# A layer with window attention, a two-way scan and memory attention: the hand-over of key tiles, the order of the last period and the rests of the side tasks

## The chip, the cores and the metric

The kernel runs on one core of one Trainium2 chip. The core has a matmul engine (TensorE, PE in the profile), a vector engine (VectorE, DVE), an engine for activation functions (ScalarE, ACT), a general one (GpSimd, POOL) and SyncE (SP), whose queue issues all of this kernel's DMA transfers. The metric is the time on the device in microseconds, from the start to the end of one launch; lower is better.

## What is computed

One encoder layer over 2048 tokens of width 1024, in float32, with three groups of heads side by side: window attention (16 query heads in 4 groups, each group with one key head), a Mamba-2 scan in both directions, and attention into 256 memory tokens.

```python
proj = rms_norm(h) @ w_in           # q, k, v, gates, z, xbc, dt, memory queries and gates
q, k = rotary(q), rotary(k)
att  = window_attention(q, k, v, sink) * silu(g_attn)      # blocks of 128 queries, keys within +-128
xbc  = silu(centred_depthwise_conv(xbc))                   # 5 taps
dt   = softplus(dt_raw + dt_bias)
y    = ssd_scan(forward) + ssd_scan(backward) + d_skip * xs
ssd  = gated_group_rmsnorm(y, z)
mem  = softmax(q_mem @ mk.T / sqrt(128)) @ mv * silu(g_mem)
h    = h + concat[att, ssd, mem] @ w_out
return rms_norm(h)
```

## The kernel before

The 2048 tokens are cut into 4 periods of 512, each of 4 blocks of 128, and worked from period c = 3 down to c = 0. The projections carry most of the matmul work. A float32 product is made as three products of a rounded high part and a low rest (`split3`: xh with wh, xl with wh, xh with wl; PE takes the rounded type `float32r` faster than float32). `split` makes the two parts, the high one on ACT (L174), the low one on DVE (L175). Weights come tile by tile through `ws` into `wh` and `wl`.

PE's order is written by the program itself, by a small planner that runs while the kernel is built. The main line (`main`) emits projections. Everything else is a *task*, a generator that emits some instructions and then yields a number, its rest. The planner keeps a clock: each matmul adds an estimate (0.216 us for a 512-column one of float32r), each transpose 0.11. After every second matmul group of the main line `tick` runs all tasks whose rest is over. `need(...)` holds the main line back until certain tasks are done: then tasks follow one another on PE without projections between them, and the planner's clock jumps ahead. There are five kinds of tasks: "att" (three at once), "mem", "ssd", "inc" and "fwd" (one each). The order on the other engines and on SP is not written by hand: a scheduler takes it from its own forecast of the times.

In a period the main line makes keys (`keys`, with the rotary step `rope`) and values, then for each head group g its query heads (`heads`), conv projections (`conv`), the gate of the scan (`z_gate`) and the memory heads (`mem_project`).

- `heads` projects the two query halves, rotates them (`rope`), writes them to DRAM (`q_d`) and reads them back in another layout into the tile `qs`; then it projects two gates, and spawns one `attention` task for each of the 4 blocks.
- `attention`: block 4c takes a place for the key tiles, starts their loads (`khh`, `kll`, `vg`), hands them to the other blocks of the group (`kv["t"]`, L498) and rests 9.0. The others wait in a loop until `kv["t"]` is there. Then each block makes 4 pairs of score matmuls into 2 banks (`s`), which DVE empties at L512 (mask, sink and row maximum `mx`); ACT takes exponentials (L520) and scales (L524). After a rest of 14.0 (9.0 for group 3 of the last period) come transposes (`t`), and 3.0 later the product with the values (`o`).
- `mem_project` loads the memory keys `mkt` and spawns `mem_attention`, which loads the memory values into the same tile once its scores are done.
- `ssd_local` makes the scan's work inside blocks, for both directions, and stores y and states. When it is done for all periods, `forward` runs block by block: it adds the state from before the block, which `incoming` prepares (`fb`, L713, L716), to y (tile `b`), multiplies by the gate (POOL, L736 and L738), squares (ACT, L739), adds pairs (DVE, L741) and rests 15.0. Then matmuls `t<-ones` make the sums (L745), DVE and POOL the factors (L747, L748, L751); after a rest of 4.0 the matmul `t<-yo` spreads them (L754), DVE scales (L756) and the block is stored to `mix_d`. The next step's `b` is the same tile.
- In the last period (c = 0) the main line makes all eight convs first and spawns `ssd_local`; then for g = 0 to 2 the memory head, the heads and one z gate, then heads 3, memory head 3 and the last z gate.
- Then the output projection: `early(c)` makes, for a block, the half of it that needs no scan, and puts it away to DRAM (`xr_d`). It is called from block 15 downward, as long as attention tasks are left. `rest_wo` loads the last seven rows of tiles of `w_out`. `out_block(c)` makes what is left of every block from 0 upward, and needs `forward(c)`.

Of the kernel before, what the change touches and what calls it, by code (L numbers as in the profile page):

```python
# [10 lines left out]
F32 = mybir.dt.float32  # L11
F32R = mybir.dt.float32r
# [24 lines left out]
def as32(ap):  # L37
    return ap.bitcast(F32)


def as32r(ap):
    return ap.bitcast(F32R)
# [3 lines left out]
def layer(ctx: ExitStack, tc: tile.TileContext, a: dict):  # L46
# [162 lines left out]
    def rope(pa, pb, tab):  # L209

        n = tab.shape[-1]
        t, u = (misc.tile([P, 2, CH], F32, name=f"rt{i}")[:, :, :n] for i in range(2))
        nc.vector.tensor_tensor(t, pa.unsqueeze(1).broadcast_to([P, 2, n]), tab[:, 1:3], ALU.mult)
        nc.vector.tensor_tensor(u, pb.unsqueeze(1).broadcast_to([P, 2, n]), tab[:, 0:2], ALU.mult)
        nc.vector.tensor_tensor(t, t, u, ALU.add)
        hi = as32r(misc.tile([P, 2, CH], F32, name="rt1")[:, :, :n])
        split(hi, as32r(t), t)
        return hi, as32r(t)
# [161 lines left out]
    def steps(s, nb, raw):  # L380
# [35 lines left out]
        nc.vector.tensor_tensor(wl, wl, dt.rearrange("p b d r -> p (b d r)"), ALU.mult)  # L416
        yield 1.5
        pt = bank(ps_t, "t")
        nc.tensor.transpose(pt[:n, :P], fl, ident)
        nc.vector.tensor_scalar(fl, fl, -1.0, None, ALU.mult)  # L420
# [60 lines left out]
    def attention(c, g, i, qs, gt, kv):  # L481
# [7 lines left out]
        if i == 4 * c:  # L489
            yield from take("kst", 1)  # L490
            kst = [ap_.tile([P, 6 * P], F32R, name=nm, bufs=2) for nm in ("khh", "kll")]
            for j in range(2):
                for u in range(2):
                    nc.sync.dma_start(as32(kst[j])[u * 64:(u + 1) * 64, :(hi + 1 - lo) * P],
                                      k_d[j, g * 32:(g + 1) * 32, :, lo * P:(hi + 1) * P].rearrange("p j t -> (p j) t"))
            vg = ap_.tile([P, 6, 64], F32, name="vg", bufs=2)
            nc.sync.dma_start(vg[:, :hi + 1 - lo], v_d[lo:hi + 1, :, g * 64:(g + 1) * 64].rearrange("b p d -> p b d"))
            kv["t"] = kst, vg  # L498
            yield 9.0
        yield from take("pm", 4)  # L500
# [22 lines left out]
        for r in range(4):  # L523
            nc.scalar.activation(pm[:, r, :w], pm[:, r, :w], AF.Copy, scale=den[:, r:r + 1])  # L524
        yield 14.0 if c or g < 3 else 9.0
        yield from take("pt", nk)
# [106 lines left out]
    def mem_project(c, xs, hd):  # L633
# [11 lines left out]
        nc.sync.dma_start(as32(mkt), mk_d[hd])  # L645
        return spawn("mem", mem_attention(c, hd, qh, ql, gm, mkt))

    def mem_attention(c, hd, qh, ql, gm, mkt):
        yield 11.0
        pms = []  # L650
        for half in range(2):
# [16 lines left out]
            pms.append(pm)  # L668
            if half:
                mvt = mkt.rearrange("p (u m d) -> p u m d", u=2, m=2)  # L670
                nc.sync.dma_start(as32(mvt), mv_d[:, :, :, hd * P:(hd + 1) * P].rearrange("u m p d -> p u m d"))
            yield 2.0 if half == 0 else 10.0
# [9 lines left out]
        for m, (tt, hi) in enumerate(pts):  # L682
            lo = misc.tile([P, 512], F32R, name="mpm", bufs=2)
            nc.vector.tensor_tensor(lo, tt, as32(hi), ALU.subtract)
            pts[m] = tt, hi, lo
        yield 2.0
        oo = bank(ps_o, "o")
# [6 lines left out]
    def incoming(c):  # L694
# [11 lines left out]
        for u in range(2):  # L706
            nc.sync.dma_start(ef[u * 64:(u + 1) * 64], ev[u].partition_broadcast(64))
        yield 5.0
        for d, st_ in enumerate((state["f"], hbt)):
# [4 lines left out]
            if d == 0:  # L714
                yield 1.0
        nc.gpsimd.tensor_tensor(ef[:, 0], ef[:, 0], ef[:, 1], ALU.add)  # L716
# [6 lines left out]
    def forward(c):  # L723
# [17 lines left out]
        nc.vector.tensor_tensor(zv[:, :, 0], zv[:, :, 0], zv[:, :, 1], ALU.add)  # L741
        yield 15.0
        pn = bank(ps_t, "t")
# [6 lines left out]
        for g in range(2):  # L750
            nc.vector.tensor_scalar(dg[:, g], ident, rn[:, g:g + 1], None, ALU.mult)  # L751
        yield 4.0
        pn = bank(ps_t, "t")
# [110 lines left out]
    fwd = []  # L864
    nz = [0] * NPER
    for c in range(NPER - 1, -1, -1):
        if c < NPER - 1:
            main(keys(c, xs))
            main(values(c, xs))
        if c == 0:  # L870
            for i in range(8):
                main(conv(c, xs, i))
            ssd_t = spawn("ssd", ssd_local(range(3, -1, -1)))
        tab = tables(CH * c, CH)
        for g in range(NG):
# [6 lines left out]
            elif c < NPER - 1:  # L882
                need(*att[c + 1, g + 2])
            if c == 0 and g < 3:
                need(mem_t)
                mem_t = main(mem_project(c, xs, g))
            att[c, g] = main(heads(c, xs, g, tab))
            if c and g == 2:
                norm_x(c - 1, rows_x(c - 1, dg))
            if c:  # L890
                main(conv(c, xs, 2 * g))
                main(conv(c, xs, 2 * g + 1))
                if g == 3:
                    spawn("ssd", ssd_local(range(4 * c + 3, 4 * c - 1, -1)))
            for _ in range(1 if c else ((1, 1, 1, 0))[g]):
                main(z_gate(c, xs, nz[c]))
                nz[c] += 1
            if c:
# [3 lines left out]
        if c == 0:  # L902
            need(mem_t)
            mem_t = main(mem_project(c, xs, 3))
            for i in range(nz[c], NG):
                main(z_gate(c, xs, i))
            fwd = [spawn("fwd", forward(b)) for b in range(NB)]
# [104 lines left out]
    while not all(t.done for ts in att.values() for t in ts):  # L1012
        if last < 4:
            need(*[t for ts in att.values() for t in ts])
        else:
            main(early(last))
            last -= 1
    rest_wo()
    for c in range(NB):
        main(out_block(c))  # L1020
# [70 lines left out]
```

## Time and profile before

| | |
|---|---|
| median of 3 runs | 1881.1 us (1878.0 to 1883.5) |
| the profiled execution | 1887.0 us, its span 1885.3 us |
| PE busy | 1770.2 us (94% of the span), 9242 matmuls |
| DVE busy | 1183.9 us (63%) |
| ACT busy | 925.1 us (49%) |
| POOL busy | 263.9 us (14%) |
| DMA (SP's queue) | 59.2% of 16 engines' span, 339.6 MB |
| mean granted clock of PE | 0.972 |

The span is the time from the first to the last instruction. Matmuls overlap, so a row's duration is longer than the distance from one start to the next. In a row of the timeline, what stands in brackets is how long the engine was idle before that instruction, and what released it. The granted clock is a share of 2.4 GHz; the clock has two levels, 2.4 and 1.2 GHz, and a mean between 1 and 0.5 is a mixture of them.

### The profile page before, as it was taken

How to read it: one execution, taken by the hardware profiler on the slowest of the kernel's cores; microseconds unless marked ns; L12 is line 12 of the kernel's file. 1: busy time of each engine (PE TensorE's matmuls, PEld its weight loads, DVE VectorE, ACT ScalarE, POOL GpSimd, SP SyncE). 2: the span in 40 equal slices, each digit the busy share in tenths (PEclk: the TensorE clock that was granted, in tenths of full speed). 3: DMA queues.
4: the chain of work that ended last, by engine and by line, in shares of the span. 5: the costliest groups of instructions: out<-in, count | busy, mean ns of one | idle time of the engine just before them, and what ended most of it. 6: DMA issues, size and time to landing. Idle time of an engine off the chain costs nothing.

```text
span 1885.3 us, 26616 instructions
## 1 busy us (share of the span) xinstructions
PE 1770.2 (94%) x9242; PEld 1441.6 (76%) x9242; DVE 1183.9 (63%) x2669; ACT 925.1 (49%) x1985; POOL 263.9 (14%) x253
## 2 busy tenths in 40 slices
PE   6789999998999999989999998999898989999998
PEld 6777878876778777866778787777676778888876
DVE  7456666686666668767576679866777543344332
ACT  6246546563756457456556665465566421111111
POOL 0000000012110000211000012211122233333220
PEclk9899999999999999999999999999999999999999
DMA  6746374577664755766474566655667765555442
GB/s 233 220 147 203 110 236 130 153 231 234 212 183 136 222 157 163 246 196 206 135 209 142 166 199 204 219 171 155 204 176 207 244 168 168 169 173 160 136 140 79
DMA packets 262695, 341.31 MB, mean 181 GB/s; under 512 B 29344, under 2 KB 171808, under 8 KB 262560
## 3 DMA queue, kind: packets, MB, share of 16 engines
q1 hardware_dynamic: 262560, 339.61, 59.2%
q8 instruction: 73, 1.20, 0.3%
q14 instruction: 62, 0.51, 0.1%
HBM read 251.20 MB, written 88.34 MB: 180 GB/s over the span
## 4 chain that ended last, share of the span: by engine, by line
PE 67%; DMA 14%; DVE 11%; ACT 4%; issue 3%; POOL 1%; SPq 1%; DVEq 0%; POOLq 0%; ACTq 0%
PE pj L156 50%; PE s L156 7%; PE o L156 5%; PE t L160 4%; DMA qs<-q_d 3%; DVE wl L175 2%; DMA q_d<-rt 2%; DMA cu<-in_x_dram 1%; DMA fb<-ef_d 1%; ACT wh L174 1%; DMA ws<-in_w_in_dram 1%; DMA mxl<-mix_d 1%; PE t L156 1%; DMA mix_d<-b 1%; DVE pm L512 1%
## 5 line engine op out<-in xcount | busy, mean ns | idle before, releaser
L156 PE MATMUL pj<-xh,wh 128*128 128x512 f32 (+2 forms) x1296 | 507.5, 392 | 1.6 <-ACT msq L852 1.6
L156 PE MATMUL pj<-xl,wh 128*128 128x512 f32 (+2 forms) x1296 | 495.9, 383 | 1.9 <-DVE xl L175 1.9
L156 PE MATMUL pj<-xh,wl 128*128 128x512 f32 (+2 forms) x1296 | 495.4, 382 | 0.1
L156 PEld LDWEIGHTS pj<-xh,wl 128*128 128x128 f32 x1296 | 247.5, 191 | 46.1 <-DVE wl L175 1.0
L156 PEld LDWEIGHTS pj<-xh,wh 128*128 128x128 f32 x1296 | 247.9, 191 | 40.9 <-issue 4.8
L156 PEld LDWEIGHTS pj<-xl,wh 128*128 128x128 f32 x1296 | 248.0, 191 | 36.8 <-DVE xl L175 2.4
L175 DVE TENSOR_TENSOR wl<-ws,wh 128x1024 fp32r<-128x1024 f32 (+2 forms) x175 | 211.4, 1209 | 96.1 <-ACT wh L174 89.5
L174 ACT CAST wh<-ws 128x1024 fp32r<-128x1024 f32 (+2 forms) x175 | 179.8, 1028 | 139.5 <-PE pj L156 96.9
L512 DVE CUSTOM_DVE_ANT_0 pm<-s,band,sink 128x384 f32<-128x384 f32 (+1 forms) x256 | 148.9, 594 | 68.6 <-PE s L156 66.9
L520 ACT ACTIVATE pm<-pm,mx 128x385 f32<-128x385 f32 (+1 forms) x256 | 151.2, 594 | 64.4 <-DVE mx L518 64.2
L608 POOL TENSOR_TENSOR b<-nat,win 128x256 f32<-128x256 f32 x64 | 44.3, 711 | 912.9 <-ACT nat L594 912.9
L156 PE MATMUL pj<-woh,mxh 128*128 128x512 f32 x416 | 171.4, 412 | 0.0
L156 PE MATMUL pj<-wol,mxh 128*128 128x512 f32 x416 | 166.1, 399 | 0.0
L156 PE MATMUL pj<-woh,mxl 128*128 128x512 f32 x416 | 166.1, 399 | 0.0
L156 PE MATMUL s<-khh,qs 128*128 128x384 f32 (+1 forms) x256 | 97.2, 380 | 55.0 <-DMA qs<-q_d 28.7
L524 ACT ACTIVATE pm<-pm,den 128x384 f32<-128x384 f32 (+1 forms) x256 | 132.9, 593 | 14.7 <-DVE den L522 14.7
L174 ACT CAST mxh<-mxl 128x512 fp32r<-128x512 f32 x64 | 39.6, 619 | 198.4 <-DMA mxl<-mix_d 94.9
L538 ACT COPY pt<-t 128x512 f32<-128x512 f32 x120 | 69.8, 582 | 103.7 <-PE t L160 103.5
L156 PEld LDWEIGHTS s<-khh,qs 128*128 128x128 f32 x256 | 50.3, 196 | 82.6 <-issue 35.1
L452 DVE SCALAR_TENSOR_TENSOR cu<-raw,cw,cu 128x512 f32<-128x512 f32 (+2 forms) x128 | 98.7, 778 | 15.6 <-ACT cu L450 14.5
L175 DVE TENSOR_TENSOR mxl<-mxl,mxh 128x512 fp32r<-128x512 f32 x64 | 50.4, 788 | 89.9 <-ACT mxh L174 89.8
L160 PE MATMUL t<-ident,pm 128*128 128x128 f32 x736 | 101.1, 274 | 2.7 <-ACT pt L538 1.8
(217 smaller groups left out, 2948.1 us busy)
## 6 DMA issues: line engine op xcount, KB each, us to landing
ws<-in_w_in_dram SPq DMA_DIRECT2D x152, 512.0 KB, 4.2
q_d<-rt SPq DMA_DIRECT2D x32, 512.0 KB, 5.5
qs<-q_d SPq DMA_DIRECT2D x32, 512.0 KB, 6.3
fb<-f_d SPq DMA_DIRECT2D x32, 512.0 KB, 4.6
mxl<-mix_d SPq DMA_DIRECT2D x64, 256.0 KB, 3.8
mix_d<-ao SPq DMA_DIRECT2D x64, 128.0 KB, 3.7
xc<-xbc_d SPq DMA_DIRECT2D x32, 256.0 KB, 3.8
st_d<-carry SPq DMA_DIRECT2D x32, 256.0 KB, 4.0
```

The costliest lines, as they stand in the source:

```text
L156: nc.tensor.matmul(out, lhsT=lhsT, rhs=rhs, start=start, stop=stop)
L160: nc.tensor.transpose(out, in_, ident)
L174: nc.scalar.copy(hi, x)
L175: (eng or nc.vector).tensor_tensor(lo, x, as32(hi), ALU.subtract)
L452: nc.vector.scalar_tensor_tensor(u, raw[:, r0 + k:r0 + k + cnt], cw[:, i, k:k + 1], u, ALU.mult, ALU.add)
L512: nc.vector.tensor_tensor_reduce(pm[:, r, :w], ss[:, :w], band[:, ms], 1.0, sink8[:, 4 * g + r:4 * g + r + 1], ALU.add, ALU.max, mx[:, r:r ...
L520: nc.scalar.activation(pm[:, r, :w + 1], pm[:, r, :w + 1], AF.Exp, bias=mx[:, r:r + 1], scale=0.125, accum_out=den[:, r:r + 1])
L524: nc.scalar.activation(pm[:, r, :w], pm[:, r, :w], AF.Copy, scale=den[:, r:r + 1])
L538: nc.scalar.copy(pts[j], tt)
L608: nc.gpsimd.tensor_tensor(xd[:, d], nat[:, 0:256].rearrange("p (r e) -> p r e", r=4), win[:, d, 4 * g:4 * g + 4].unsqueeze(2).broadcast_to ...
```

## The change

- **Key tiles.** Block 4c now rests 10.0 first and then hands the tiles over, so that all four blocks of a group wait.
- **Last period.** The convs are no longer made first: five stand after heads 0, three after heads 1, then `ssd_local` is spawned. z gate 0 stands after them, z gate 1 after heads 2, gates 2 and 3 after heads 3; every memory head stands before its heads. Every block of this period rests 10.0 between scores and transposes.
- **Memory values** have a tile of their own (`mvt`), loaded together with the keys.
- **Rests.** `steps` 1.5 to 2.0, memory attention 2.0 to 3.0, `incoming` 5.0 to 7.0 and 1.0 to 1.5, `forward` 15.0 to 11.0 and 4.0 to 5.5.
- **Rope.** Where a table has at most 320 columns (the two key halves of the first period worked), each of the three tiles is a buffer of `xp` (4 of them) instead of `rt0` and `rt1` (one each).
- **Early blocks.** After `rest_wo`, more early halves are made until `forward(1)` is done. In the orders there are two before and five after (blocks 15 to 11).

```diff
@@ rope
-        t, u = (misc.tile([P, 2, CH], F32, name=f"rt{i}")[:, :, :n] for i in range(2))
+        small = 2 * n <= XW
+
+        def half(name):
+            if small:
+                return misc.tile([P, XW], F32, name="xp", bufs=4)[:, :2 * n].rearrange("p (j t) -> p j t", j=2)
+            return misc.tile([P, 2, CH], F32, name=name)[:, :, :n]
+
+        t, u = half("rt0"), half("rt1")
...
-        hi = as32r(misc.tile([P, 2, CH], F32, name="rt1")[:, :, :n])
+        hi = as32r(half("rt1"))
@@ attention
             nc.sync.dma_start(vg[:, :hi + 1 - lo], v_d[lo:hi + 1, :, g * 64:(g + 1) * 64].rearrange("b p d -> p b d"))
+            yield 10.0
             kv["t"] = kst, vg
-            yield 9.0
...
-        yield 14.0 if c or g < 3 else 9.0
+        yield 14.0 if c else 10.0
@@ mem_project
+        mvt = misc.tile([P, 2, 2, P], F32R, name="mvt")
+        nc.sync.dma_start(as32(mvt), mv_d[:, :, :, hd * P:(hd + 1) * P].rearrange("u m p d -> p u m d"))
@@ mem_attention
-            if half:
-                mvt = mkt.rearrange("p (u m d) -> p u m d", u=2, m=2)
-                nc.sync.dma_start(as32(mvt), mv_d[:, :, :, hd * P:(hd + 1) * P].rearrange("u m p d -> p u m d"))
...
-        yield 2.0
+        yield 3.0
         oo = bank(ps_o, "o")
@@ incoming
-        yield 5.0
+        yield 7.0
...
             if d == 0:
-                yield 1.0
+                yield 1.5
@@ forward
-        yield 15.0
+        yield 11.0
         pn = bank(ps_t, "t")
...
-        yield 4.0
+        yield 5.5
         pn = bank(ps_t, "t")
@@ the main line
-        if c == 0:
-            for i in range(8):
-                main(conv(c, xs, i))
-            ssd_t = spawn("ssd", ssd_local(range(3, -1, -1)))
...
-            if c == 0 and g < 3:
+            if c == 0:
                 need(mem_t)
                 mem_t = main(mem_project(c, xs, g))
             att[c, g] = main(heads(c, xs, g, tab))
...
+            for i in range(2 * g, 2 * g + 2) if c else ((0, 1, 2, 3, 4), (5, 6, 7), (), ())[g]:
+                main(conv(c, xs, i))
+                if i == 7:
+                    ssd_t = spawn("ssd", ssd_local(range(4 * c + 3, 4 * c - 1, -1)))
+            for i in (g,) if c else ((), (0,), (1,), (2, 3))[g]:
+                main(z_gate(c, xs, i))
...
 rest_wo()
+    while last > 3 and not fwd[1].done:
+        main(early(last))
+        last -= 1
     for c in range(NB):
         main(out_block(c))
```

PE, the first scores of the kernel (period 3, group 0; qs_927 is the query tile, pj_981 the group's last gate, pj_1025 the first half of conv 0, pj_1138 the second half of conv 1). Before:

```order
L156 MATMUL pj_1025<-xl_383,wh_1020 128x320
L156 MATMUL pj_1025<-xh_382,wl_1021 128x320
L156 MATMUL s_1044<-khh_1032,qs_927 128x384
L156 MATMUL s_1044<-kll_1033,qs_927 128x384
L156 MATMUL s_1052<-khh_1032,qs_927 128x384
L156 MATMUL s_1052<-kll_1033,qs_927 128x384
```

After:

```order
L156 MATMUL pj_1138<-xl_395,wh_1107 128x320
L156 MATMUL pj_1138<-xh_394,wl_1108 128x320
L156 MATMUL s_1155<-khh_1032,qs_927 128x384
L156 MATMUL s_1155<-kll_1033,qs_927 128x384
L156 MATMUL s_1163<-khh_1032,qs_927 128x384
L156 MATMUL s_1163<-kll_1033,qs_927 128x384
```

The scores have moved from 6 conv matmuls after the gate to 84 conv matmuls after it.

PE, the last head group (qs_13526 before, qs_13650 after; s<-mkt is memory attention, o<-b1 and s<-b2 the scan, pj_14159 and pj_14160 an early block of the output projection). Before:

```order
L160 MATMUL t_14025<-ident_105,pm_13769 128x128 x4
L156 MATMUL s_14035<-khh_13777,qs_13526 128x256
L156 MATMUL s_14035<-kll_13778,qs_13526 128x256
L156 MATMUL s_14039<-mkt_13909,qh_13901 128x256 x2
L156 MATMUL s_14039<-mkt_13909,ql_13902 128x256
L156 MATMUL s_14039<-mkt_13909,qh_13901 128x256 x2
L156 MATMUL s_14039<-mkt_13909,ql_13902 128x256
L160 MATMUL t_14056<-ident_105,pm_13769 128x128 x4
L156 MATMUL s_14062<-khh_13777,qs_13526 128x256
L156 MATMUL s_14062<-kll_13778,qs_13526 128x256
L156 MATMUL s_14066<-khh_13777,qs_13526 128x256
L156 MATMUL s_14066<-kll_13778,qs_13526 128x256
```

After:

```order
L156 MATMUL s_14229<-xc_13962 128x128
L156 MATMUL pj_14159<-wh_14103,mxh_14163 128x512
L156 MATMUL pj_14159<-wl_14104,mxh_14163 128x512
L156 MATMUL pj_14159<-wh_14103,mxl_14161 128x512
L156 MATMUL pj_14160<-wh_14103,mxh_14163 128x512
L156 MATMUL pj_14160<-wl_14104,mxh_14163 128x512
L156 MATMUL pj_14160<-wh_14103,mxl_14161 128x512
L156 MATMUL s_14253<-khh_13901,qs_13650 128x384
L156 MATMUL s_14253<-kll_13902,qs_13650 128x384
L156 MATMUL pj_14159<-wh_14109,mxh_14163 128x512
L156 MATMUL pj_14159<-wl_14110,mxh_14163 128x512
L156 MATMUL pj_14159<-wh_14109,mxl_14161 128x512
```

The last scores, which stood in a run of 60 rows without a projection, now stand between the matmuls of an early block.

DVE, one step of the forward scan in the output projection (b1 is the scan's square, fb the incoming state, rn the sum of a block, xr and rs the output). Before:

```order
L713 TENSOR_TENSOR fb_15134<-s_15161,fb_15134 128x512
L713 TENSOR_TENSOR fb_15134<-s_15173,fb_15134 128x512
L741 TENSOR_TENSOR b1_15118<-b1_15118 128x2x128
L995 TENSOR_TENSOR xr_15095<-pj_15083,xr_15095 128x512
L747 TENSOR_SCALAR rn_15229<-t_15226 128x2
```

After (L741, L713 and L747 of before are L747, L719 and L753 there):

```order
L747 TENSOR_TENSOR b1_15668<-b1_15668 128x2x128
L998 TENSOR_TENSOR rs_15721<-s2_15720 128x1
L999 TENSOR_SCALAR rs_15721<-rs_15721 128x1
L719 TENSOR_TENSOR fb_15684<-s_15751,fb_15684 128x512
L1003 SCALAR_TENSOR_TENSOR xr_15560<-xr_15560,rs_15721,nwo_14157 128x512 x2
L753 TENSOR_SCALAR rn_15766<-t_15763 128x2
```

The sum over pairs has moved ahead of the passes over fb.

## Rows read from the trace of the kernel before

**Rows 1.** Waits of PE: line, releaser: us in total, times, longest us

```profile
PE s L156 <- DMA qs<-q_d: 28.7, 7, 7.5
PE s L156 <- DVE mx L512: 24.6, 17, 3.5
...
PE t L156 <- DVE b L741: 6.0, 1, 6.0
PE o L156 <- issue: 5.6, 1, 5.6
PE pj L156 <- DVE rt L214: 5.3, 1, 5.3
```

**Rows 2.** Stretches: us, PE, PEld, DVE, ACT, POOL busy, clock, DMA share, GB/s

```profile
112.00:460.00 348.00, 331.31 (x1854) 276.55 (x1854) 233.56 (x521) 197.94 (x436) 18.37 (x19) 0.98 0.59 179
460.00:800.00 340.00, 325.92 (x1714) 259.63 (x1715) 234.84 (x550) 201.99 (x444) 30.48 (x30) 0.97 0.61 188
800.00:1120.00 320.00, 302.71 (x1599) 242.81 (x1598) 221.29 (x517) 194.21 (x426) 24.25 (x25) 0.97 0.58 176
1120.00:1412.00 292.00, 276.24 (x1459) 221.24 (x1458) 218.03 (x543) 163.83 (x362) 54.54 (x52) 0.98 0.63 191
1412.00:1480.00 68.00, 56.98 (x313) 44.05 (x313) 49.30 (x113) 42.54 (x94) 19.19 (x14) 0.90 0.71 222
1480.00:1530.00 50.00, 43.64 (x216) 35.08 (x213) 24.06 (x38) 16.09 (x25) 14.75 (x12) 0.93 0.71 205
1530.00:1800.00 270.00, 267.44 (x1263) 221.11 (x1261) 106.70 (x219) 46.49 (x93) 84.15 (x75) 0.99 0.56 163
```

**Rows 3.** Timeline of PE at period 2's first scores: start us, us, instruction

```profile
463.38 0.66 PE L156 MATMUL s<-khh,qs 128*128 128x384 f32 x1 [7.54 <-DMA qs<-q_d]
...
465.23 0.63 PE L156 MATMUL pj<-xl,wh 128*128 128x512 f32 x1
465.65 0.63 PE L156 MATMUL pj<-xh,wl 128*128 128x512 f32 x1
...
468.23 0.40 PE L156 MATMUL pj<-xl,wh 128*128 128x512 f32 x1
468.47 0.39 PE L156 MATMUL pj<-xh,wl 128*128 128x512 f32 x1
```

**Rows 4.** Timeline of PE, 24 conv matmuls apart, at period 3's first convs

```profile
129.47 0.31 PE L156 MATMUL pj<-xh,wh 128*128 128x320 f32 x1
...
132.99 0.31 PE L156 MATMUL pj<-xh,wh 128*128 128x320 f32 x1
```

**Rows 5.** Timelines of PE, SP, POOL and DVE: one step of the forward scan

```profile
1650.26 0.59 PE L156 MATMUL t<-yo,ones 128*128 128x256 f32 x2
1652.04 0.36 SPq L758 DMA_DIRECT2D mix_d<-b  x1
1654.37 0.36 SPq L731 DMA_DIRECT2D b<-y_d  x1
1657.46 1.31 POOL L736 TENSOR_TENSOR b<-b,fb 128x512 f32<-128x512 f32 x1 [1.26 <-DMA b<-y_d]
1660.83 0.59 DVE L741 TENSOR_TENSOR b<-b 128x256 f32<-128x256 f32 x1 [3.19 <-ACT b L739]
1667.75 0.50 PE L156 MATMUL t<-ones,b 128*128 128x1 f32 x4
```

**Rows 6.** Timelines of PE and DVE: a step under loads, and a slow one

```profile
1524.42 0.77 PE L156 MATMUL t<-ones,b 128*128 128x1 f32 x3 [6.02 <-DVE b L741]
...
1767.98 0.59 PE L156 MATMUL t<-yo,ones 128*128 128x256 f32 x2
1783.85 0.43 DVE L741 TENSOR_TENSOR b<-b 128x256 f32<-128x256 f32 x1 [7.14 <-ACT b L739]
```

**Rows 7.** Timeline of DVE: the same two passes at two places

```profile
1656.23 1.41 DVE L1008 SCALAR_TENSOR_TENSOR xr<-xr,rs,nwo 128x512 f32<-128x512 f32 x2 [0.67 <-POOL rs L1005]
...
1682.90 3.22 DVE L1008 SCALAR_TENSOR_TENSOR xr<-xr,rs,nwo 128x512 f32<-128x512 f32 x2 [2.12 <-POOL rs L1005]
```

More of the change, by code (lines that the diff above doesn't have):

```diff
@@ L416, in steps @@
         nc.vector.tensor_tensor(wl, wl, dt.rearrange("p b d r -> p (b d r)"), ALU.mult)
-        yield 1.5
+        yield 2.0
         pt = bank(ps_t, "t")
-        nc.tensor.transpose(pt[:n, :P], fl, ident)
+        tr(pt[:n, :P], fl)
         nc.vector.tensor_scalar(fl, fl, -1.0, None, ALU.mult)
@@ L645, in mem_project, with mem_attention @@
         nc.sync.dma_start(as32(mkt), mk_d[hd])
-        return spawn("mem", mem_attention(c, hd, qh, ql, gm, mkt))
-    def mem_attention(c, hd, qh, ql, gm, mkt):
+        mvt = misc.tile([P, 2, 2, P], F32R, name="mvt")
+        nc.sync.dma_start(as32(mvt), mv_d[:, :, :, hd * P:(hd + 1) * P].rearrange("u m p d -> p u m d"))
+        return spawn("mem", mem_attention(c, hd, qh, ql, gm, mkt, mvt))
+    def mem_attention(c, hd, qh, ql, gm, mkt, mvt):
         yield 11.0
@@ L864, in layer @@
     fwd = []
-    nz = [0] * NPER
     for c in range(NPER - 1, -1, -1):
@@ L889, in layer @@
                 norm_x(c - 1, rows_x(c - 1, dg))
[L890 to L897, printed above, removed]
+            for i in range(2 * g, 2 * g + 2) if c else ((0, 1, 2, 3, 4), (5, 6, 7), (), ())[g]:
[4 more added lines that the diff above has]
+                main(z_gate(c, xs, i))
             if c:
@@ L902, in layer @@
         if c == 0:
[L903 to L906, printed above, removed]
             fwd = [spawn("fwd", forward(b)) for b in range(NB)]
```

## The prediction, made before the changed kernel was run

> **What bounds the kernel.** I read the waits of TensorE (PE) first. The list of its waits [rows 1] is short, and nearly all of it is attention: 28.7 us in 7 waits for the query tile qs to come back from DRAM, 24.6 us in 17 waits for the VectorE (DVE) step L512 that empties a bank of scores. Each other line is one wait. Then the stretches [rows 2]: PE is busy for 95 to 96% of the time in the three stretches of 112 to 1120 us and idle for 16.7, 14.1 and 17.3 us in them; from 1120 to 1412 us it is idle for 15.8 us, from 1412 to 1480 us for 11.0 of 68 us, from 1480 to 1530 us for 6.4. PE's work is the same before and after: both orders have 7340 rows of it. So the change is worth what it does to these gaps, and to the slow clock behind them. That clock is seen in PE's timeline at 463 us [rows 3]: after the 7.54 us wait the granted clock is at the lower level (1.2 GHz), and two 512-column matmuls start 0.42 us apart, where 3 us later they start 0.24 us apart (2.4 GHz). From 463.38 to 468.23 us PE started 8 score matmuls and 7 of the projection; at 0.147 x 384 / 320 = 0.176 [rows 4] and 0.24 us these take 3.1 us at the upper level, and they took 4.85: 1.8 us lost.
>
> **Query waits.** Before, block 4c of a head group hands its key tiles over as soon as their loads are issued and rests 9.0 itself; the blocks beside it start their scores at once. On PE only 6 conv matmuls stand between the last gate matmul of the group and the first score; after, in the same place of the first period, it is 24 + 24 + 24 + 12 = 84 (four tiles, pj_1025 to pj_1138, of which two rows are shown). At 24 matmuls in 132.99 - 129.47 = 3.52 us [rows 4], 0.147 us each, the 78 more are 11.4 us. The longest of the seven waits is 7.5 us, so qs lands 3.9 us before it is asked for, and all seven should go: 28.7 us, and 1.8 us of clock for each of the three long ones (6.9, 7.5, 7.3). Together **-34**; if the clock were not given back, -29. What is late next is DVE, below.
>
> **The pile of side tasks at the end of attention.** Before, two projections are made after the last heads, then PE has 60 rows of scores, transposes, scan and memory attention (5651 to 5710 of its order) with no projection between them; 12 are shown in front. After, the longest such run has 13 rows. The stretch of 1412 to 1480 us lost 11.0 us idle, and its granted clock was 0.90 where the stretch before had 0.98: some 16% more of 68 us, 11 us, at half rate, of which I take half as busy time, 5.4 us doing the work of 2.7. Of these 13.7 us I leave 3: **-11** (-5 to -14).
>
> **Last period.** Eight conv projections in a row, with five DVE passes each, become five and three between heads. Of the 14 us idle there that are no query wait, the largest is 5.6 us in front of the memory attention's last matmuls [rows 1]. I take half: **-7** (0 to -14). The separate mvt tile only loads earlier. In this period the blocks of groups 0 to 2 get 10 instead of 14 between scores and transposes. Group 3 ran on 9.0, and no wait of PE for the softmax's scaling (L524) is in the list. I take 0.
>
> **Periods 3 to 1.** Outside the query waits 48.1 - 26.8 = 21.3 us are idle there, mostly L512 queued behind other DVE work. The scores move 11 us later, from the gates into the convs; the 16 pairs of a group stand less in lockstep. A gain and a loss are both possible: **-3** (-15 to +15).
>
> **The forward scan** is where the change takes cover away. A step runs from the matmul t<-yo to the next t<-ones. The chain between [rows 5]: store of the old block (1652.04), load of the next y (1654.37, in use at 1657.46), two GpSimd (POOL) operations, a square, and L741, done at 1661.42: 11.2 us after t<-yo at 1650.26. PE came to t<-ones at 1667.75, 17.5 us after it, so 6 us were spare. There 66 output matmuls and two groups of scan matmuls stood between (rows 6150 to 6219 of PE's order); after, 48 and one group (rows 6204 to 6254 and every later step). At about 0.9 us for a group the 66 took 15.7 us, 0.238 each, and the new spacing is 48 x 0.238 + 0.9 = 12.3 us. That leaves 1.1 us. The DVE order helps: L741 now stands ahead of both passes over fb, while before it stood behind them in some steps. The bounds are 0 and the slow step [rows 6], t<-yo at 1767.98 to L741 done at 1784.28, 16.3 us, in a quarter of 15 steps: 4 x 4 = 16. I take **+5** (0 to +16). The steps under the w_out loads had one wait of 6.0 us [rows 6]; these loads now meet the scan's second step, and I take the same wait again: 0 (-6 to +4).
>
> **Edits at nothing.** Three more early blocks (five instead of two) write and read 3 x 0.5 MB each way, in stretches whose DMA share is 0.56 to 0.71 [rows 2], and add two DVE passes each, where DVE has room. The first rope's smaller tiles spare the second rope its wait for the k_d store (5.3 us in front of a values matmul [rows 1]). But the second rope still waits for its table, and the split wl_691, which that values projection needs, now stands behind it in DVE's queue: 0 (-5 to +2). At the start a load of mvt now stands ahead of the k_d stores in SyncE's queue, but nothing asks for k_d before the first scores. Longer rests (2.0, 3.0, 7.0, 1.5, 5.5) only move work back into projections.
>
> **Sum**: -34 - 11 - 7 - 3 + 5 = -50. The profiled execution took 1887.0 us, 5.9 more than the median of 1881.1. So it would take 1837, and the median would be **1831**.
>
> **Rivals.**
> (1) Slower: the forward scan becomes the bound. If each step's chain is as long as the slow one, 16.3 us against 12.3, PE waits 4 us in 15 steps, 60 us, and loses up to 1.8 us of clock each time, 27: -55 + 87 = +32, **1913**. To be slower by 0.3% takes 61 us in 15 steps, 4.1 each; with the clock that is a chain of 14.6 us at every step. For it: the spare time falls from 6 to 1 us. Against: typical chains are 11.2, and the DVE order is better. 7%.
> Where DVE and POOL meet, two passes of L1008 took 3.22 us instead of 1.41 [rows 7]. The Trainium skill ("SBUF — State Buffer", section "SBUF: two separate sides") says that GpSimd and a DVE operation with two SBUF inputs share a port pair, which one holds for its whole instruction while the other blocks. By that rule scan steps packed closer collide more often: 1.8 us more make a chain of 13.0, 0.7 us of waiting in 15 steps, 10 instead of 5, and 1836. It does not decide the sign alone.
> (2) The wait moves to DVE: the scores fall among conv's DVE passes, and each of the 16 head groups pays two new L512 waits of the present mean, 24.6 / 17 = 1.45 us: 46 us, -4 in all, **1877**. For it: these waits are there now. Against: convs stood beside later scores before as well. 10%.
> (3) The queries come later than before, since SyncE's queue issues them behind other loads: half of the -34 stays away, **1848**. 13%.
> (4) The L512 waits shrink too and the rest reaches its better end (-15, -14, -14, scan 0): -77, **1804**. 17%.
> The forecast itself, 1815 to 1846: 53%.
>
> **Chances and range.** About 0.3% (5.6 us) is what a measurement of this kernel can tell from no change. Faster: 53 + 17 + 13 and a little of (2), 0.85. Same: 0.07. Slower: (1) and the end of (2), 0.08. The range has to reach (4) and (3) and a part of (2): 1798 to 1868.
>
> **What would show it.** The line qs<-q_d leaves PE's waits; the stretch of the last scores has a clock of 0.97 or more and under 4 us idle; the idle time of 112 to 1120 us falls from 48 to about 20 us; in the scan the time from t<-yo to t<-ones is 12 to 13 us and waits for L741 add up to under 16 us. I am wrong if those exceed 40 us, or if L512 waits grow beyond 50.

## The result, and the profile after

The changed kernel takes 1928.3 us (median of 4 runs, 1921.5 to 1937.0) against 1881.1: 1.0264 times the time before, 95% interval 1.0229 to 1.0298. The forecast was 1831, faster. The profiled execution is the slowest of the four, 1937.0 us; its span is 1935.3, which is 50.0 longer than before.

Of these 50 us, 26.8 are idle time of TensorE (PE) and 23.2 are busy time, for the same number of matmuls; the mean granted clock fell from 0.972 to 0.962 (0.967 to 0.971 in the other three runs). The first line of the page, after:

```profile
PE 1793.4 (93%) x9242; PEld 1450.2 (75%) x9242; DVE 1186.1 (61%) x2675; ACT 923.0 (48%) x1985; POOL 260.9 (13%) x253
```

PE's waits after (line, releaser: us in total, times, longest), to be read against [rows 1]; L519 is L512 of before, L747 is L741, L545 is L538, L601 is L594:

```profile
PE s L156 <- DVE mx L519: 33.9, 32, 4.4
PE t L160 <- ACT nat L601: 15.0, 6, 6.0
PE t L156 <- DVE b L747: 11.6, 7, 2.4
...
PE pj L156 <- ACT mxh L174: 8.8, 1, 8.8
PE pj L156 <- DVE wl L175: 8.7, 4, 4.9
PE o L156 <- ACT pt L545: 6.0, 3, 4.5
PE t L160 <- ACT pt L545: 4.9, 3, 4.4
PE o L156 <- ACT pt L686: 4.5, 1, 4.5
...
PE t L156 <- DVE yo L757: 3.0, 1, 3.0
...
PE s L156 <- DMA qs<-q_d: 0.6, 1, 0.6
```

The 28.7 us for the query tile are gone, down to 0.6. In their place stand, most of all, waits that ACT releases: the scan's copy `nat`, the attention's copies `pt` (L686 is that of the memory attention), the split `mxh`. Over the whole list these are 52 us, 16 before. Waits that DVE releases rose from 55 to 79 us; those for the row maximum have nearly doubled in number. The first three stretches of [rows 2], after:

```profile
112.00:460.00 348.00, 326.94 (x1809) 271.51 (x1808) 227.67 (x503) 193.46 (x429) 15.29 (x15) 0.97 0.57 173
460.00:800.00 340.00, 316.19 (x1648) 249.60 (x1647) 230.61 (x540) 199.04 (x439) 30.82 (x30) 0.97 0.60 187
800.00:1120.00 320.00, 305.41 (x1548) 241.03 (x1546) 218.30 (x491) 181.74 (x385) 26.91 (x26) 0.97 0.56 171
```

PE is idle for 59.5 us in them, where the prediction expected the 48 to fall to about 20. Since the kernel does not stand at the same point at each of these bounds, the same work no longer lies in the same stretch. A better ruler is a mark that every variant passes with the same projections behind it: in PE's timeline, the first matmul of each period's values projection (`pj<-wh,xh` of 128x272). It stands at 62.35, 407.08, 756.12 and 1104.10 us before, at 63.38, 398.89, 769.79 and 1128.04 after. The table gives the distances between these marks in one profiled run of each kernel, then the time from the last mark to PE's last matmul, and the time from the last mark to the first `t<-yo` of the forward scan. Single runs differ by a few us: the changed kernel, e3, e4 and e7 have the same program up to the last mark, and their distances differ by up to 4.7.

| kernel | period 3 | period 2 | period 1 | last part | scan's first t<-yo |
|---|---|---|---|---|---|
| before | 344.7 | 349.0 | 348.0 | 773.6 | 372.2 |
| changed | 335.5 | 370.9 | 358.2 | 800.0 | 412.8 |
| e1 hand-over alone | 338.5 | 361.6 | 349.8 | 771.5 | 358.0 |
| e2 hand-over undone | 334.9 | 355.1 | 348.6 | 792.2 | 407.9 |
| e3 rests undone | 332.9 | 370.8 | 357.5 | 794.6 | 415.6 |
| e4 last period undone | 330.8 | 371.6 | 355.7 | 769.8 | 347.7 |
| e5 later hand-over at both ends only | 341.6 | 355.5 | 344.9 | 768.9 | 351.4 |
| e6 later hand-over, 4c later still | 335.0 | 355.2 | 355.3 | 769.7 | 360.4 |
| e7 last period, rests undone | 332.7 | 371.4 | 357.2 | 763.6 | 347.4 |
| e8 last period, hand-over undone | 333.6 | 352.9 | 343.5 | 787.2 | 370.1 |
| e9 last period alone | 343.2 | 351.8 | 346.7 | 789.9 | 414.3 |
| e10 late hand-over only in the last period | 334.6 | 351.5 | 348.8 | 761.4 | 364.5 |
| e11 before, no scaling | 342.4 | 351.4 | 344.5 | 765.2 | 366.6 |
| e12 hand-over, no scaling | 334.7 | 358.3 | 344.1 | 762.6 | 349.9 |
| e13 changed, no scaling | 334.3 | 360.3 | 349.5 | 786.5 | 401.9 |
| e14 half way | 338.2 | 351.3 | 343.2 | 769.3 | 352.2 |

So period 3 gained 9 us, periods 2 and 1 lost 22 and 10, the last part lost 26. That makes two losses to explain: one in the middle periods, one at the end.

### What PE waits for in period 2

PE's timeline at the longest new wait (start us, us, instruction, in brackets the idle time before it and its releaser):

```profile
505.73 0.83 PE L160 MATMUL t<-ident,pm 128*128 128x128 f32 x4
512.57 1.12 PE L160 MATMUL t<-ident,pm 128*128 128x128 f32 x4 [6.01 <-ACT nat L601]
513.34 0.78 PE L156 MATMUL pj<-xh,wh 128*128 128x512 f32 x1
513.91 0.63 PE L156 MATMUL pj<-xl,wh 128*128 128x512 f32 x1
514.34 0.63 PE L156 MATMUL pj<-xh,wl 128*128 128x512 f32 x1
```

PE wants a second bank for transposes. Such a bank is held by the scan's transposes until ACT has copied them to `nat`. They were made at 502.4 us, 9.6 us before that copy began (PE):

```profile
502.43 0.49 PE L160 MATMUL t<-ident,xc 128*128 128x128 f32 x3
```

ACT's timeline up to the copy:

```profile
504.06 2.12 ACT L531 ACTIVATE pm<-pm,den 128x384 f32<-128x384 f32 x4
506.09 0.61 ACT L281 ACTIVATE cu<-cu 128x512 f32<-128x512 f32 x1
506.61 0.19 ACT L281 ACTIVATION_READ_ACCUMULATOR cu<-cu 128x1 f32 x1
506.70 1.03 ACT L174 CAST wh<-ws 128x1024 fp32r<-128x1024 f32 x1
507.63 0.57 ACT L647 CAST qh<-pj 128x512 fp32r<-128x512 f32 x1
508.11 1.04 ACT L174 CAST wh<-ws 128x1024 fp32r<-128x1024 f32 x1
509.06 0.59 ACT L206 ACTIVATE th<-pj 128x512 f32<-128x512 f32 x1
509.55 2.13 ACT L531 ACTIVATE pm<-pm,den 128x384 f32<-128x384 f32 x4
511.57 0.57 ACT L633 COPY carry<-s 128x512 f32<-128x512 f32 x1
512.04 0.48 ACT L601 COPY nat<-t 128x384 f32<-128x384 f32 x1
512.41 0.59 ACT L545 COPY pt<-t 128x512 f32<-128x512 f32 x1
```

No bracket stands in these rows: ACT was never idle. It worked in its order, and the copy of 0.48 us that PE needs stands behind two scalings of the softmax (L531, 2.1 us each), two weight casts, a square for the next period's norm (L281) and more. Over the span ACT is 48% busy; here it is full. The 2.4 GHz clock is lost too: behind the wait the 512-column matmuls start 0.43 us apart.

At the border between periods 3 and 2 the same queue stands still for a load (ACT's, then SyncE's timeline):

```profile
435.38 1.04 ACT L174 CAST wh<-ws 128x1024 fp32r<-128x1024 f32 x1 [10.09 <-DMA ws<-in_w_in_dram]
436.33 0.58 ACT L545 COPY pt<-t 128x512 f32<-128x512 f32 x1
```

```profile
418.78 0.59 SPq L634 DMA_DIRECT2D st_d<-carry  x1
424.20 0.33 SPq L563 DMA_DIRECT2D carry<-st_d  x1
...
428.37 0.33 SPq L636 DMA_DIRECT2D hb_d<-state  x1
...
429.27 0.46 SPq L181 DMA_DIRECT2D ws<-in_w_in_dram  x1
```

The weights' load is issued behind the scan's stores and its reload of the state: the reload (L563) waits 4.7 us for the store before it, the next store (L636) 3.3 us for the state that GpSimd makes. ACT's cast waits 10.1 us for it, and `pt`, which stands behind the cast, costs PE 4.5 us. Before, ACT waited there too, for 6.3 us, but no attention copy stood behind it. With the later attention one does.

### The profile page after: what moved, and what is told of

Read it like the earlier page. It is cut to its first block, busy times and chain, and to the rows that moved or that the text cites. A ratio compares the mean times of both kernels' runs of the same rounds, so it can differ in the third digit from the quotient of the medians.

```text
span 1935.3 us, 26623 instructions
## 1 busy us (share of the span) xinstructions
PE 1793.4 (93%) x9242; PEld 1450.2 (75%) x9242; DVE 1186.1 (61%) x2675; ACT 923.0 (48%) x1985; POOL 260.9 (13%) x253
## 4 chain that ended last, share of the span: by engine, by line
PE 64%; DVE 11%; DMA 11%; ACT 7%; issue 3%; POOL 2%; SPq 1%; POOLq 0%; DVEq 0%; ACTq 0%
PE pj L156 47%; PE s L156 7%; PE o L156 5%; PE t L160 5%; DVE wl L175 2%; DMA mix_d<-b 2%; ACT wh L174 1%; DVE pm L519 1%; DMA ws<-in_w_in_dram 1%; DMA cu<-in_x_dram 1%; ACT pm L527 1%; DMA b<-y_d 1%; DVE cu L459 1%; DMA xn_d<-xp 1%; PE t L156 1%
## 5 line engine op out<-in xcount | busy, mean ns | idle before, releaser
L519 DVE CUSTOM_DVE_ANT_0 pm<-s,band,sink 128x384 f32<-128x384 f32 (+1 forms) x256 | 150.3, 595 | 42.0 <-PE s L156 40.1
L545 ACT COPY pt<-t 128x512 f32<-128x512 f32 x120 | 70.0, 584 | 136.8 <-PE t L160 136.6
L531 ACT ACTIVATE pm<-pm,den 128x384 f32<-128x384 f32 (+1 forms) x256 | 132.8, 594 | 4.0 <-DVE den L529 4.0
L160 PE MATMUL t<-ident,pm 128*128 128x128 f32 x736 | 105.2, 279 | 17.7 <-ACT nat L601 13.0
L160 PEld LDWEIGHTS t<-ident,pm 128*128 128x128 f32 x736 | 87.8, 143 | 40.2 <-ACT nat L601 14.1
L156 PE MATMUL o<-pt,vg 128*64 128x256 f32 x736 | 96.0, 394 | 6.4 <-ACT pt L545 6.0
```

The lines of the kernel that those rows point to most:

```text
L156: nc.tensor.matmul(out, lhsT=lhsT, rhs=rhs, start=start, stop=stop)
L160: nc.tensor.transpose(out, in_, ident)
L519: nc.vector.tensor_tensor_reduce(pm[:, r, :w], ss[:, :w], band[:, ms], 1.0, sink8[:, 4 * g + r:4 * g + r + 1], ALU.add, ALU.max, mx[:, r:r ...
L545: nc.scalar.copy(pts[j], tt)
```

## The experiments

Ratios are to the kernel before, run on the same chip beside it.

### e1: the hand-over alone

```diff
# in the kernel before
+            yield 10.0
             kv["t"] = kst, vg
-            yield 9.0
```

> The kernel before with one edit: block 4c rests 10.0 and then hands the key tiles over (it no longer rests 9.0 after it). Theory A (the wait moves): the 28.7 us for qs go, but the whole softmax of a group comes 11 us later, into the next projections, and PE then waits as long for copies and row maxima that stand behind other work in the queues of ACT and DVE: 1870 to 1895. Theory B (the hand-over gains what was forecast, other edits lose it): 1845 to 1860.

Measured: 1895.3 us, 1.0072 (1.0045 to 1.0099). Theory A, just past its upper end. No wait for `qs` is left, and yet the edit that was to bring 34 us costs 14.

### e2: the changed kernel with the old hand-over

```diff
# in the changed kernel
-            yield 10.0
             kv["t"] = kst, vg
+            yield 9.0
```

> The changed kernel with the old hand-over (tiles handed over at once, then a rest of 9.0). Theory A: about the same or a little better than the changed kernel, 1905 to 1930. Theory B: 1950 to 1965, since the qs waits come back and nothing is saved.

Measured: 1901.9, 1.0100 (1.0066 to 1.0134). Theory A, a little better than its range. The `qs` waits are back (34.0 us in 9), and the kernel is 1.6% shorter than the changed one. Periods 2 and 1 fall to 355.1 and 348.6.

### e3: the scan's rests undone

```diff
# in the changed kernel
@@ incoming
-        yield 7.0
+        yield 5.0
...
-                yield 1.5
+                yield 1.0
@@ forward
-        yield 11.0
+        yield 15.0
...
-        yield 5.5
+        yield 4.0
```

> The changed kernel with the four rests of the scan as before (forward 15.0 and 4.0, incoming 5.0 and 1.0). Theory S (the scan's chain has become the bound: the part of the output projection lost 16 us more than before): the waits for L747 go, 1908 to 1915. Rival (the scan's loss is bound elsewhere, since what is saved per step comes back at the end as scan work without cover): 1925 to 1935.

Measured: 1930.8, 1.0250 (1.0210 to 1.0290), no difference from the changed kernel. The rival: the waits for L747 are gone, but the last two output blocks now wait 3.2 and 8.1 us for the scan's result, whose last `t<-yo` comes at 1899 instead of 1861 us. With the late start, what the old rests save in waits at each step they cost at the end.

### e4: the last period's order undone

```diff
# in the changed kernel
-            for i in range(2 * g, 2 * g + 2) if c else ((0, 1, 2, 3, 4), (5, 6, 7), (), ())[g]:
...
+        if c == 0:
+            for i in range(8):
+                main(conv(c, xs, i))
+            ssd_t = spawn("ssd", ssd_local(range(3, -1, -1)))
...
-        yield 14.0 if c else 10.0
+        yield 14.0 if c or g < 3 else 9.0
```

The z gates and the memory heads go back to their old places as well.

> The changed kernel with the last period in the old order (eight convs first, scan task after them, the old rests of 14.0 and 9.0). Theory P (the new order loses some 9 us in the last period and gives nothing back): 1915 to 1922. Rival (the new order gains: it thins the pile at the end of attention): 1935 to 1945.

Measured: 1903.1, 1.0109 (1.0079 to 1.0139): 1.6% below the changed kernel, more than theory P asked for. The last part is 769.8 instead of 800.0 us, and the scan's first `t<-yo` comes 347.7 instead of 412.8 us after the mark.

### e5: the later hand-over only where it seemed to pay

```diff
# in the kernel before
+            if c == 0 or (c == NPER - 1 and g == 0):
+                yield 10.0
+                kv["t"] = kst, vg
+            else:
                 kv["t"] = kst, vg
                 yield 9.0
```

> The kernel before, with the later hand-over only in the last period and in the first group of the first period worked (c = 3, g = 0); everywhere else the old one. From the hand-over alone: its first period was 6 us shorter than before and the part from the last period's values on 2 us shorter, the period between lost 12.6. Theory A (the later hand-over gains where ACT and DVE have room and loses in the middle periods): 1868 to 1878. Rival (gain and loss can't be taken apart by place, each new order falls as it falls): 1880 to 1895.

Measured: 1881.3, 0.9996 (0.9974 to 1.0017). The rival: no gain that can be measured. Most of the loss of the middle periods is gone (700.4 us together, 711.4 in e1, 697.0 before), but so is half of what e1 had gained in period 3 (341.6 us there).

### e6: the later hand-over, and block 4c not with the others

```diff
# in the kernel before
+            yield 10.0
             kv["t"] = kst, vg
             yield 9.0
```

> The kernel before, where block 4c rests 10.0, hands over, and then rests 9.0 more, so that it does not start with the others. Theory L (the loss comes from the blocks of a group going in lockstep, their softmax filling ACT at once): the qs waits go and no wait takes their place, 1855 to 1870. Theory D (the loss comes from the delay: the group's tail falls into the next projections, whose casts stand in the same queues): as the hand-over alone or worse, 1888 to 1905.

Measured: 1890.3, 1.0053 (1.0035 to 1.0072). Theory D. The waits for the row maximum (26.4 us in 25) and for `pt` (15.1 in 6) are there as well. Three of the blocks still start together; that the fourth went with them is not what cost.

### e7: last period and rests undone

In the changed kernel, the edits of e3 and e4 together.

> The changed kernel with the last period in its old order and the four rests of the scan as before. With the old order alone it took 1903, and its first t<-yo came at 1471 instead of 1541 us. Theory S2 (the shorter rests cost waits for L747 in themselves; with an early scan start the old rests are free): the 14.8 us of waits for L747 go, 1890 to 1897. Rival (these waits are cover for others): 1900 to 1908.

Measured: 1897.1, 1.0095 (1.0061 to 1.0130). The median lies at the upper end of S2's range, and one wait of 6.3 us for L747 is left of 14.8 in 10; but against e4's 1.0109 the gain is inside both intervals. That the rests cost something with an early scan is likely from the waits, not shown by the time.

### e8: last period and hand-over undone

In the changed kernel, the edits of e2 and e4 together.

> The changed kernel with the last period in its old order and the old hand-over; what is left of the change are the smaller rope tiles, the memory values' own tile, the rests and the extra early blocks. Theory A (the two losses, 26 and 25 us, are independent): 1876 to 1882, as before the change. Rival (they overlap: the later hand-over gains in the old last period): 1886 to 1900.

Measured: 1894.0, 1.0073 (1.0048 to 1.0098). The rival: the two losses are not independent. Periods 3 to 1 together are 11.7 us shorter than before, but the last part takes 787.2 us where e4, with the later hand-over, takes 769.8. In the old order of the last period the later hand-over gains, in the stretch from the mark to the last projection (306.2 us against 325.8).

### e9: the new last period alone

In the kernel before, the new order of the last period and its rests (the edit of e4 the other way round).

> The kernel before with the new order of the last period alone (convs after heads 0 and 1, z gates later, memory heads first, rests of 10.0). Theory P2 (the new order delays the scan's last local part by some 60 us, so the forward scan begins late and ends with the program or after it): first t<-yo 30 to 60 us later than before, 1900 to 1912. Rival (the delay is only dear with the shorter rests): 1878 to 1890.

Measured: 1895.8, 1.0089 (1.0057 to 1.0121). Slower, a little less than P2 said. The scan starts late as it said: the first `t<-yo` comes 414.3 us after the mark instead of 372.2, the last one 21 us before the end, and an output block waits 7.6 us for its input at 1881 us. That wait is the smaller part of the loss, though; the larger one lies before the scan begins (see the last period, below).

### e10: what is left when the losing parts are taken back

```diff
# in the changed kernel, with the edits of e3 and e4
-            yield 10.0
-            kv["t"] = kst, vg
+            if c:
+                kv["t"] = kst, vg
+                yield 9.0
+            else:
+                yield 10.0
+                kv["t"] = kst, vg
```

> The changed kernel with the old order of the last period, the old rests of the scan, and the later hand-over kept in the last period only. From pieces of the runs: start to the last period's values 1096 us (as with last period and hand-over undone), from there to the end 764 us (as with last period and rests undone), 8 us to the launch's end: 1866 to 1872, faster than both kernels. Rival (the pieces are not independent): 1880 to 1890.

Measured: 1870.5, 0.9943 (0.9925 to 0.9960): faster than both kernels. PE's waits there:

```profile
PE s L156 <- DMA qs<-q_d: 33.0, 6, 11.3
```

Of the kernels here that compute the whole layer the fastest is one that keeps 33 us of waits for `qs`.

### e11 and e12: ACT relieved, without and with the hand-over

```diff
# in the kernel before (e11), and in e1 (e12)
-        for r in range(4):
-            nc.scalar.activation(pm[:, r, :w], pm[:, r, :w], AF.Copy, scale=den[:, r:r + 1])
```

> The kernel before without the scaling of the softmax (L524 left out, so that the output lacks the division by the row sums): 256 operations, about 132 us of ACT's work, are gone. Alone it is the base for the next run: 1855 to 1880.

> The hand-over alone, also without the scaling of the softmax. Theory A (what replaces the qs waits is ACT's queue in the middle of the attention): with ACT relieved the hand-over pays after all, 15 to 25 us less than the run without scaling and the old hand-over. Rival D (ACT isn't what binds; the delay costs on DVE or in the order): 8 to 16 us more than it, as with the scaling.

Measured: 1877.9 (0.9989, 0.9965 to 1.0012) and 1868.9 (0.9936, 0.9900 to 0.9972). The two leave out the division by the row sums. Some 120 us less work on ACT is worth nothing measurable in the kernel before, and 1.4% with the later hand-over; without it the hand-over is a gain of 9 us instead of a loss of 14. That is theory A's sign, at half its size. The same wait in e12 (PE, then ACT):

```profile
497.03 0.66 PE L160 MATMUL t<-ident,pm 128*128 128x128 f32 x4 [2.20 <-ACT nat L592]
```

```profile
493.19 1.04 ACT L174 CAST wh<-ws 128x1024 fp32r<-128x1024 f32 x1
494.13 0.57 ACT L638 CAST qh<-pj 128x512 fp32r<-128x512 f32 x1
494.60 1.04 ACT L174 CAST wh<-ws 128x1024 fp32r<-128x1024 f32 x1
495.55 0.59 ACT L206 ACTIVATE th<-pj 128x512 f32<-128x512 f32 x1
496.04 0.57 ACT L624 COPY carry<-s 128x512 f32<-128x512 f32 x1
496.50 0.48 ACT L592 COPY nat<-t 128x384 f32<-128x384 f32 x1
```

It is the row of casts and copies seen above without the scalings, and the wait is 2.2 us where e1 had 4.2. ACT is not all of it: period 2 still takes 358.3 us against 351.4 in e11, and the waits for L512 are 34.5 us in 28.

### e13: the changed kernel without the scaling

The same lines left out of the changed kernel.

> The changed kernel without the scaling of the softmax (the output lacks the division by the row sums). Without it the kernel before was 4 us shorter, the hand-over alone 26 us. Theory A (ACT's queue is the cause of the hand-over's loss in the whole change too): 20 us or more below the changed kernel, 1895 to 1908; what is left over the kernel before is the last period and the scan's late start. Rival (the loss of the whole change in the middle periods has another cause, such as the memory values' tile or the weights' loads): 1918 to 1926.

Measured: 1901.5, 1.0133 (1.0097 to 1.0169), 1.3% below the changed kernel. Theory A: ACT's queue is what the later attention meets in the whole change too. No wait of PE for the scaling itself (L531) stands in the changed kernel's list, so what the edit relieves is the queue, not a wait for its result. Periods 2 and 1 fall by 10.6 and 8.7 us. Of the 13.5 us that the last part gains, 13.0 lie before its last projection (340.4 to 327.4 us from the mark; 315.1 to 310.8 in the kernel before). What is left over e11 is mostly the last part, 786.5 against 765.2.

### e14: half way

```diff
# in the changed kernel, with the edits of e3 and e4
-            yield 10.0
+            yield 4.0 if c else 10.0
             kv["t"] = kst, vg
+            if c:
+                yield 5.0
```

> The changed kernel with the old order of the last period and the old rests of the scan; the hand-over stays at 10.0 in the last period, and in the other periods block 4c rests 4.0, hands over and rests 5.0 more. Theory M (the qs waits and the crowding at ACT each grow with the delay, and half way costs less than either end): the 33 us for qs fall to about 15 and ACT's waits stay small, 1855 to 1866. Rival (what the shorter delay saves for qs it loses at ACT and DVE): 1868 to 1882.

Measured: 1875.3, 0.9988 (0.9968 to 1.0008). The rival: a shorter delay saves the `qs` waits, and waits for ACT come instead (`pt` 11.2 us in 6, the longest 6.8).

## Why the prediction was wrong, step by step

**Query waits, -34.** They left, all but 0.6 us, as worked out. That this shortens the kernel was the wrong part: e1 alone is 14 us longer.

**Periods 3 to 1, -3 (-15 to +15).** This is the step that failed, together with the last period, below. The prediction moved the scores 11 us later and asked only what DVE (L512) would make of it; ACT's queue, which the rest of the attention meets later too, it put at nothing. The later half now falls into stretches that hold other bursts: the weight casts of the next projections, the squares of the next norm, the scan's copies. The three periods together were to shrink by about 35 us and grew by 22.9 (1064.6 against 1041.7). Taking 120 us of work off ACT turns the hand-over's loss of 14 us into a gain of 9 (e1, e12) and takes 19.3 us off periods 2 and 1 of the changed kernel (e13). Of ACT the prediction says once, of the last period, that no wait for the scaling is in the list of waits. That list says who is late now, not who is late next. The Trainium skill ("Perfetto Trace Analysis", section "Identifying the Most-Contended Engine") takes the occupancy of ScalarE as a fair measure of how close it is to its limit. Taken over the span it does not show this place: at 48% there, ACT had no idle row between 504 and 513 us, and PE waited 6.0 us for it.

**The clock.** The prediction counted 1.8 us for each of three long waits. Measured, 26.8 us more idle time came with 23.2 us more busy time. Worked out from the mean granted clock, PE stood at the lower level for an estimated 147 us of the span, 106 before (2 x 0.038 x 1935.3 and 2 x 0.028 x 1885.3, the lower level being half the upper); half of the difference, 21 us, is nearly all of the 23.2. How much of it belongs to the many short waits was not taken apart.

**The pile of side tasks, -11.** The side tasks were spread out, and the stretch of the last scores gained as worked out: the prediction asked for a clock of 0.97 or more and under 4 us idle, and from the end of the wait shown below it is 0.97 and 1.3 us. After:

```profile
1478.00:1546.00 68.00, 66.66 (x355) 50.74 (x354) 39.29 (x95) 35.38 (x76) 14.70 (x13) 0.97 0.69 211
```

But 8.8 us of the gain are lost just ahead of it. The pile had covered the loads of the early block's inputs: before, 30 us lay between the last projection and that block's first matmul, after 9 us. Without it PE waits for them (PE, then ACT):

```profile
1477.50 0.80 PE L156 MATMUL pj<-wh,mxh 128*128 128x512 f32 x1 [8.82 <-ACT mxh L174]
```

```profile
1476.83 1.38 ACT L174 CAST mxh<-mxl 128x512 fp32r<-128x512 f32 x2 [7.04 <-DMA mxl<-mix_d]
```

What would be late next was named for the queries (DVE), but not for the early block.

**Last period, -7.** Wrong by sign. The new order costs 1.6% in the changed kernel (e4) and 0.9% alone (e9). Most of this lies before the scan begins. From the last mark to the last projection (before, changed, e4, e9):

```profile
1104.10:1419.20 315.10, 298.82 (x1615) 241.56 (x1614) 236.16 (x585) 183.28 (x411) 59.13 (x56) 0.98 0.64 195
1128.04:1468.40 340.36, 314.64 (x1672) 250.97 (x1672) 243.41 (x598) 188.86 (x428) 53.39 (x53) 0.95 0.59 179
1122.95:1429.10 306.15, 297.13 (x1618) 239.98 (x1618) 236.37 (x587) 182.58 (x410) 57.60 (x56) 0.99 0.64 199
1103.71:1451.30 347.59, 319.52 (x1710) 256.14 (x1708) 250.53 (x634) 192.61 (x441) 57.27 (x57) 0.96 0.60 180
```

PE is idle there for 16.3, 25.7, 9.0 and 28.1 us, and its clock is 0.95 and 0.96 with the new order, 0.98 and 0.99 with the old; the rest of the length is matmuls of side tasks that fall into the stretch. The longest line of waits in the changed kernel is again the row maximum, 9.5 us in 8 (0.9 in 2 in e4); every other line is 4.5 us or less. From the last projection to PE's end the idle time differs less: 20.0 us before, 24.8 in the changed kernel, 25.0 in e4.

The new order also makes the scan begin later: with the convs behind the first two heads, `ssd_local` is spawned later, and the first `t<-yo` falls 41 to 42 us later after the mark (changed, e9), 65 us later than in e4. In the changed kernel that is not shown to cost anything: the last `t<-yo` stands 67 us before PE's end, and no output block waits for the scan. With the old rests it does cost, 7.6 us of waits at the end of e9 and 11.3 of e3. In this term the prediction looked at the gaps of the old order; it asked neither what the scores would meet between the convs nor when the scan can begin.

**Forward scan, +5 (0 to +16).** This term was about right. The waits are 14.6 us (L747 and L757), against 8.6 before (L741 and L751): 6.0 more. From `t<-yo` to `t<-ones` it is 12.4 to 15.2 us, where 12.3 was worked out; steps take 19.4 to 25.1 us, where 23.5 was usual before. A slow one (PE, SP, SP, DVE, PE):

```profile
1774.92 0.59 PE L156 MATMUL t<-yo,ones 128*128 128x256 f32 x2
1776.70 0.37 SPq L764 DMA_DIRECT2D mix_d<-b  x1
1782.83 0.36 SPq L737 DMA_DIRECT2D b<-y_d  x1
1789.25 0.59 DVE L747 TENSOR_TENSOR b<-b 128x256 f32<-128x256 f32 x1 [4.63 <-ACT b L745]
1789.99 0.99 PE L156 MATMUL t<-ones,b 128*128 128x1 f32 x4 [2.42 <-DVE b L747]
```

The chain was sized from a step in which the next load followed the store after 2.3 us [rows 5]; here it follows after 6.1, since it waits for the store to land. e3 shows that with the late start both spacings take as long.

**Edits at nothing.** e10, which keeps the smaller rope tiles, `mvt`, the other rests and the early blocks, is 0.57% below the kernel before; its hand-over in the last period was worth nothing in e5, together with that of the first group. So these small edits probably gain, most in period 3 (334.6 against 344.7 us), where the wait of 5.3 us for `rt` [rows 1] is gone. Which of them does was not tried apart.

**The rivals.** Rival (2), that the wait moves, had the right idea, but the waits for the row maximum grew by 9.3 us, not by 46, and no rival named ACT. Rival (1), the scan as the bound, did not come: its waits grew by 6.0 us, and it is done 67 us before the end. Neither of the two signs of being wrong that the prediction names came either: the waits for L747 are 11.6 us, not over 40, and those for L519 33.9, not over 50. Of the Trainium skill's rule on the shared port pair ("SBUF — State Buffer", section "SBUF: two separate sides"), cited there, the traces show no more with the steps packed closer: of the 32 passes of L1003 (L1008 before) 2 took over 0.85 us, 3 before, each beside a GpSimd operation; the median is 748 ns, 746 before.

**What stays open.** Why the later hand-over gains 17 us in the last part in its old order (e8 against e4) and none that could be measured in e5; what of period 2's loss is DVE's, since e12 took away ACT's part alone; and how the loss of the last period's projections is shared between DVE and ACT, of which e13 shows only that ACT has a part.

## What to carry to other kernels

A wait that is hidden behind other work is only gained if the work that moves with it lands where its engines have room: look, in the trace, at the queue of each engine at the new place, busy or not for ten microseconds at a time, not at its share of the span. An in-order queue that mixes small copies, on which the matmul engine waits, with long softmax passes and with casts that wait for loads is the first place to look. And of a chain near the end of the program ask when a reordering lets it start, but count a late start as a loss only where the trace shows someone waiting for it: here the scan began 41 us later, and only with its old rests did the last output blocks wait.

## What was not expected of the hardware

Nearly half of the lost time is not idle time, in the executions profiled. The same 9242 matmuls took 1793.4 instead of 1770.2 us of busy time; behind a wait of 6.0 us the 512-column matmuls start 0.43 us apart, against 0.23 ahead of it. And 256 operations that fill ACT for some 120 us (925.1 us busy in the kernel before, 804.9 without them) cost nothing measurable in one order of the program and 1.4% in another.
